# First ConvFFN of a two-layer hybrid block: from an interleaved up and down to an up phase of quarter products and a down phase summed in PSUM

## The chip, the core and the metric

The kernel runs on one core of a Trainium2 chip. The metric is the device time of one execution in microseconds; a time "before" or "after" is the median over several executions. TensorE multiplies matrices, VectorE (DVE) and ScalarE (ACT) work on tiles elementwise, GpSimd (POOL) does some elementwise work and issues some DMAs, and SyncE (SP) issues most DMAs. SBUF is the on-chip memory, PSUM the banks into which TensorE accumulates.

## The reference, cut to what matters

Two layers follow one another; tokens are 256 context tokens and 1024 latent tokens of width 1024. Layer 0 mixes by attention, layer 1 by a state-space model, whose input projection reads all tokens. Behind each mixer stands the same gated ConvFFN:

```python
def conv_ffn(u, w_up, b_up, conv_w, conv_b, w_down, b_down):
    hdn = dwconv_centered(u @ w_up + b_up, conv_w, conv_b)   # 3 taps along the tokens
    val, gate = jnp.split(hdn, 2, axis=-1)                    # D_FF = 2816 each
    return (val * jax.nn.silu(gate)) @ w_down + b_down

def post_norm_layer(h, y_mix, mods, ln_g, ln_b, ffn):
    h = layer_norm(ALPHA * h + mods[2][:, None] * y_mix, ln_g[0], ln_b[0])
    f = conv_ffn(modulate(h, mods[3], mods[4]), *ffn)
    return layer_norm(ALPHA * h + mods[5][:, None] * f, ln_g[1], ln_b[1])   # "LN2" is the outer one
```

Layer 0 needs the ConvFFN for all 1280 tokens, layer 1 for the latents alone. All data are 32-bit floats. Each factor of a product is split into a high part (a copy in TensorE's reduced 32-bit type) and a low part (the rest), and a product is three matmuls: high x high, low x high, high x low.

## The kernel before, in words

The feature dimension of a ConvFFN is cut into 22 blocks of 128 (`NFB`), called feature tiles here, each with a value half and a gate half. The tokens are cut into ten tiles of 128, of which 0 and 1 are context.

**First ConvFFN** (`conv_ffn`). For a feature tile, `up` multiplies the value block and then the gate block of `w_up` with the modulated tokens `uh`, `ul`, in three chunks of 512, 512 and 256 tokens (line 1428, names `wush`, `wusl`). ScalarE copies each chunk from PSUM with the bias. `conv` makes the three taps: one on ScalarE, two on VectorE (L1909 to L1911, tile `cv`). `gated` makes silu on ScalarE and the product on VectorE (L1917), and splits the result into `gh`, `gl`, which stay in SBUF. Between the matmuls of the next tile's `up`, a function `unit` places the down products of the tile before (L1930), twenty of three matmuls, and VectorE adds each result from PSUM into an accumulator `y` in SBUF (L1944). Behind the last tile comes an LN2 stage that is written out by hand: `ffn_out`, `ffn_norm` (L2155 normalizes), the transposes of `emit_u` (L352), and, for each latent tile, the first 512 columns of the SSM's z product (`z_out`, L2186).

**Second ConvFFN** (`lat_up` and `Down`). The latents alone are multiplied in quarters: `w_up`'s block in four quarters (two halves by two halves of the input width), the tokens in four, and seven products in place of eight, from sums `s1` to `s4` of weight quarters and `t1` to `t4` of token quarters (the first three tiles take all eight products, while the sums of the tokens are being made). Each summed quarter needs a high half (`hi`, a ScalarE copy, L1529) and a low half (`lo`, a VectorE subtraction, L1534). The gated tile goes to DRAM (`g1_d`), and `Down` reads it back for groups of four token tiles, whose eight PSUM banks are summed over all 22 feature tiles (L1793).

**Order.** In both parts instructions stand on each engine's queue in the order of the program (`manual_schedule`), and a waiting instruction holds all that stand behind it on its engine. SyncE and GpSimd are such queues too, for the DMAs that they issue. In the background of the first ConvFFN a generator (`gen_ffn0`) places the adaLN products of layer 1 (L266) and then `gen_residual`: GpSimd makes `alpha * h` plus bias terms for ten token tiles (L2035 to L2049), with one tile buffer `t4k`: load from `z_d`, multiply, add, store to `r0_d`. `conv_ffn` takes seven steps of it per block of `up`, two blocks to a feature tile.

**What the change touches.** `up_mul`, `FirstBlock`, `FirstPair`, `lat_up` (lines 1426 to 1742), `Down` (L1744 to L1817), `conv_ffn` and the LN2 stage (L1835 to L2248), the block list and the z blocks of the in-projection (L2531, L2629, L2652), and the call of the second ConvFFN (L2948).

Of the kernel before, what the change touches and what calls it, by code (L numbers as in the profile page):

```python
# [74 lines left out]
def body(nc, tc, a, out):  # L75
# [330 lines left out]
    r0_d = dp.tile([NTOK, D], F32, name="r0d")  # L406
# [1019 lines left out]
    def up_mul(pt, w, uh, ul, k, o, n):  # L1426
        for j, (w_, u_) in enumerate(((w[0], uh), (w[0], ul), (w[1], uh))):
            T.matmul(pt, lhsT=w_[:, k, :], rhs=u_[:, k, o:o + n], start=(k + j == 0), stop=(k == KB - 1 and j == 2))  # L1428

    class FirstBlock:  # L1430

        def __init__(self, pool, l, chunks):
            self.pool, self.src, self.chunks, self.pts = pool, a['ffn_w_up'][l], chunks, []

        def load(self):
            self.raw = self.pool.tile([P, KB, P], F32, name="wuf")
            dma(out=self.raw, in_=self.src.rearrange("(k p) n -> p k n", p=P)[:, :, 0:P])

        def split(self):
            self.hl = [self.pool.tile([P, KB, P], F32R, name="wus" + c) for c in "hl"]  # L1440
            split(*self.hl, self.raw, eng=G)

        def product(self, ci, uh, ul):

            o, n = self.chunks[ci]
            self.pts.append(pp.tile([P, 512], F32, name="mm", bufs=4))
            for k in range(KB):
                up_mul(self.pts[ci][:, :n], self.hl, uh, ul, k, o, n)


    class FirstPair:

        def __init__(self, pool, l, chunks):
            self.pool, self.src, self.chunks, self.pts = pool, a['ffn_w_up'][l].rearrange("(k p) n -> p k n", p=P), chunks, []

        def load(self):
            self.raw = [self.pool.tile([P, KB, P], F32, name="wu" + c) for c in "vg"]
            for i in range(2):
                dma(out=self.raw[i], in_=self.src[:, :, i * DFF:i * DFF + P])

        def split(self):
            self.hl = {}
            for j, nm in enumerate(("a11", "a12")):
                self.hl[nm] = [self.pool.tile([P, 4, P], F32R, name=nm + c) for c in "hl"]
                split(*self.hl[nm], self.raw[0][:, 4 * j:4 * j + 4, :], eng=G)

        def product(self, ci, uh, ul):
# [14 lines left out]
    def lat_up(l, uh, ul, c0, pre, g_d, gq, plain, dpool, ones_ahead):  # L1482
# [20 lines left out]
        raw, A, ops, cv = {0: pre.raw}, {}, {}, {}
        ops[0] = dict(pre.hl)

        def load(n):
            if n < NFB:
                raw[n] = [pre.pool.tile([P, KB, P], F32, name="wu" + c) if n % 2 == 0 else rpool.tile([P, KB, P], F32, name="wu" + c) for c in "vg"]
                for i in range(2):
                    dma(out=raw[n][i], in_=w3[:, :, i * DFF + n * P:i * DFF + (n + 1) * P])  # L1510

        def src(n, nm):
            if nm[0] == 'a':
                return raw[n]['12'.index(nm[1])][:, 4 * '12'.index(nm[2]):4 * '12'.index(nm[2]) + 4, :]
            return A[n, nm]

        def summed(n, nm):

            if n < NFB and n not in plain:
                x, y, f = {'s1': ('a21', 'a22', ALU.add), 's2': ('s1', 'a11', ALU.subtract), 's3': ('a11', 'a21', ALU.subtract), 's4': ('a12', 's2', ALU.subtract)}[nm]  # L1520
                A[n, nm] = rpool.tile([P, 4, P], F32, name="s", bufs=3)
                V.tensor_tensor(out=A[n, nm], in0=src(n, x), in1=src(n, y), op=f)

        def hi(n, nm):
            if n < NFB:
                pool = pre.pool if nm in ('a11', 'a12') else opool
                t = [pool.tile([P, 4, P], F32R, name=('s1' if nm == 'a21' else nm) + c) for c in "hl"]
# [1581 lines left out]
```

## Time and profile before

| | |
|---|---|
| median of 3 executions | 3134.17 us (3133.34 to 3135.21) |
| the profiled execution | 3128.95 us, span 3127.0 us, mean granted TensorE clock 0.979 |
| TensorE busy | 2990.9 us, 96% |
| VectorE busy | 2188.2 us, 70% |
| ScalarE busy | 1276.2 us, 41% |
| GpSimd busy | 686.7 us, 22% |
| first ConvFFN and LN2 stage | first up product at 858, last at 1817, in-projection from 1911 us on |
| second ConvFFN, up phase | 2438 to 2861 us, its feature tiles from 2513 on without a wait of TensorE |

An engine's busy time is a sum over the whole span; what a stage is bound by has to be read from that stage. "Idle before" of a group names the instruction that ended the wait. Matmuls overlap, so a single one's duration (0.39 us for 512 columns) is longer than the pitch at which they follow each other. The granted clock is a share of TensorE's full 2.4 GHz, and its other level is 1.2 GHz.

### The profile page before, as it was taken

To read this page: it belongs to the slowest core of one execution; us is meant where nothing else is said; L and a number is where in the kernel's file an instruction comes from. 1 tells how busy PE (TensorE), PEld (TensorE's weight loads), DVE (VectorE), ACT (ScalarE), POOL (GpSimd) and SP (SyncE) were. 2 spreads that over 40 slices of the span, in tenths; PEclk is the share of its full clock that TensorE was granted. 3 is DMA by queue.
4 is the path that set the end of the run, shared out by engine and by line. 5 is a ranking of instruction groups with operands and counts; after the bars stand their busy time and mean duration, and the time that the engine had idled before them with its cause. 6 is when DMAs were issued, how large, how long until landed. Compare 5 with 4: busy or idle time off the path is not lost.

```text
span 3127.0 us, 39837 instructions
## 1 busy us (share of the span) xinstructions
PE 2990.9 (96%) x15188; PEld 2420.9 (77%) x15188; DVE 2188.2 (70%) x3270; ACT 1276.2 (41%) x2176; POOL 686.7 (22%) x664
## 2 busy tenths in 40 slices
PE   8999999999999999999999969999879999999998
PEld 4776788898888877887788858786648788887786
DVE  2278867887755656565676694966988788886776
ACT  3421257785532222222222345244435555554342
POOL 1046511321100000000442250213654000001412
PEclk9999999999999999999999989999889999999999
DMA  8635569333332222222332233331043222223653
GB/s 277 216 108 162 175 177 210 94 85 110 121 102 81 75 70 79 81 78 64 102 121 81 68 106 96 95 95 43 1 141 101 80 82 81 83 85 120 224 169 108
DMA packets 284883, 347.85 MB, mean 111 GB/s; under 512 B 24135, under 2 KB 207861, under 8 KB 284692
## 3 DMA queue, kind: packets, MB, share of 16 engines
q1 hardware_dynamic: 266820, 289.15, 30.6%
q0 software_dynamic: 11808, 40.94, 3.7%
q10 hardware_dynamic: 6064, 15.21, 1.6%
q8 instruction: 120, 1.97, 0.3%
q14 instruction: 71, 0.58, 0.1%
HBM read 264.74 MB, written 74.20 MB: 108 GB/s over the span
## 4 chain that ended last, share of the span: by engine, by line
PE 75%; DVE 14%; DMA 4%; ACT 3%; issue 2%; POOL 0%; SPq 0%; ACTq 0%; DVEq 0%; POOLq 0%
PE mm L1428 18%; PE mm L1478 12%; PE tr L1930 6%; PE mm L1353 6%; PE mm L2657 4%; PE bg L1930 3%; PE mm L878 3%; PE s L1094 3%; PE mm L1793 3%; PE bg L1152 3%; PE mm L978 2%; PE tr L1793 1%; PE bg L1793 1%; PE bg L266 1%; PE bg L1131 1%
## 5 line engine op out<-in xcount | busy, mean ns | idle before, releaser
L1428 PE MATMUL mm<-uh,wush 128*128 128x512 f32 (+1 forms) x1056 | 378.1, 358 | 0.0
L1428 PE MATMUL mm<-uh,wusl 128*128 128x512 f32 (+1 forms) x1056 | 374.6, 355 | 2.2 <-DVE wusl L90 2.1
L1428 PE MATMUL mm<-ul,wush 128*128 128x512 f32 (+1 forms) x1056 | 375.1, 355 | 0.0
L1889 ACT ACTIVATE hb<-mm,ffc 128x512 f32<-128x512 f32 x132 | 80.9, 614 | 559.3 <-PE mm L1428 559.3
L1944 DVE TENSOR_TENSOR y<-y,tr 128x512 f32<-128x512 f32 x266 | 181.3, 686 | 153.7 <-PE tr L1930 152.9
L1428 PEld LDWEIGHTS mm<-uh,wush 128*128 128x128 f32 x1056 | 199.2, 189 | 57.2 <-issue 23.6
L1428 PEld LDWEIGHTS mm<-ul,wush 128*128 128x128 f32 x1056 | 199.1, 189 | 35.2
L1428 PEld LDWEIGHTS mm<-uh,wusl 128*128 128x128 f32 x1056 | 198.9, 188 | 31.8 <-DVE wusl L90 3.0
L1102 DVE TENSOR_REDUCE mx<-s 128x1 f32<-128x1280 f32 x120 | 150.6, 1272 | 49.8 <-PE s L1094 49.8
L1944 DVE TENSOR_TENSOR y<-y,bg 128x512 f32<-128x512 f32 x134 | 91.8, 685 | 89.8 <-PE bg L1930 89.7
L2028 POOL DMA_DIRECT2D g<-in_ln_g_dram x1 | 0.6, 599 | 623.1 <-DVE y L1944 623.1
L1107 ACT ACTIVATE p<-s,mx 128x1280 f32<-128x1280 f32 x96 | 127.9, 1332 | 19.1 <-DVE r L1112 13.0
L978 PE MATMUL mm<-uh,wsh 128*128 128x512 f32 (+1 forms) x320 | 125.7, 393 | 0.0
L1152 PE MATMUL bg<-vt,wt 128*128 128x128 f32 x960 | 125.5, 278 | 0.0
L372 DVE TENSOR_TENSOR ul<-utmp,uh 128x512 fp32r<-128x512 f32 x76 | 55.1, 747 | 91.2 <-ACT uh L370 91.0
L1152 PEld LDWEIGHTS bg<-vt,wt 128*128 128x128 f32 x960 | 116.6, 193 | 0.7
L978 PE MATMUL mm<-ul,wsh 128*128 128x512 f32 (+1 forms) x320 | 114.5, 358 | 0.0
L978 PE MATMUL mm<-uh,wsl 128*128 128x512 f32 (+1 forms) x320 | 114.4, 357 | 0.0
L1930 PE MATMUL tr<-wdsh,gh 128*128 128x512 f32 x280 | 110.8, 396 | 0.0
L1930 PE MATMUL tr<-wdsl,gh 128*128 128x512 f32 x280 | 109.6, 392 | 1.2 <-DVE wdsl L90 1.2
L1930 PE MATMUL tr<-wdsh,gl 128*128 128x512 f32 x280 | 110.7, 396 | 0.0
L1553 POOL DMA_DIRECT2D g1d<-cvv x22 | 11.8, 537 | 441.8 <-DVE cvv L1552 441.8
(824 smaller groups left out, 8559.2 us busy)
## 6 DMA issues: line engine op xcount, KB each, us to landing
adaw<-in_ada_w_dram SPq DMA_DIRECT2D x40, 1024.0 KB
wdf<-in_ffn_w_down_dram SPq DMA_DIRECT2D x66, 512.0 KB
wuf<-in_ffn_w_up_dram SPq DMA_DIRECT2D x44, 512.0 KB
wuv<-in_ffn_w_up_dram SPq DMA_DIRECT2D x22, 512.0 KB
wug<-in_ffn_w_up_dram SPq DMA_DIRECT2D x22, 512.0 KB
g1d<-cvv POOLq DMA_DIRECT2D x22, 512.0 KB, 2.9
gf<-g1d SPq DMA_DIRECT2D x44, 256.0 KB
wf<-in_attn_w_in_dram SPq DMA_DIRECT2D x18, 512.0 KB
```

The source lines that it names most:

```text
L878: T.matmul(pt[:, :n], lhsT=u_[:, tt, k, :], rhs=w_[:, k, o:o + n], start=(i == 0), stop=(i == 23))
L978: T.matmul(pt.rearrange("p (t n) -> p t n", n=P), lhsT=w_[:, k, :], rhs=u_[:, o // P:(o + n) // P, k, :], start=(k + i == 0), stop=(k == K ...
L1102: V.reduce_max(t.mx[:, i, q:q + 1], t.s[i][:, c0:c0 + nk], axis=X, negate=True)
L1107: S.activation(t.p[i][q], t.s[i][:, c0:c0 + nk], AF.Exp, bias=t.mx[:, i, q:q + 1], accum_out=t.sm[:, i, q:q + 1])
L1152: T.matmul(t.po[:, P:2 * P], lhsT=t.wt[0][:, b, :], rhs=vt[:, b, :], start=(b == 0), stop=(b == NTT - 1))
L1353: T.matmul(pt, lhsT=u_[:, k, :], rhs=w_[k][:, hc], start=(k + i == 0), stop=(k == K - 1 and i == 2))
L1428: T.matmul(pt, lhsT=w_[:, k, :], rhs=u_[:, k, o:o + n], start=(k + j == 0), stop=(k == KB - 1 and j == 2))
L1478: T.matmul(pt, lhsT=w_[:, k, :], rhs=u_[:, k, :], start=start and k + j == 0, stop=stop and k == 3 and j == 2, skip_group_check=True)
L1793: T.matmul(pt, lhsT=g_[:, c], rhs=w_[:, hc], start=start and i == 0, stop=stop and i == 2)
L1930: T.matmul(pt, lhsT=g_[:, c0:c0 + P], rhs=w_[:, hc], start=(start and j == 0), stop=(stop and j == 2))
L1944: V.tensor_tensor(out=yacc[ti][:, hc], in0=yacc[ti][:, hc], in1=pt, op=ALU.add)
L2657: T.matmul(pt[0:M, :n], lhsT=w_[:, k, :], rhs=u_[:, k, o:o + n], start=(k + i == 0), stop=(k == KB - 1 and i == len(pairs) - 1))
```

## The change

The first ConvFFN takes the two-phase form of the second. `lat_up` becomes `ffn_up`, which both call.

- Up: the latents take the seven quarter products (all eight in the first three tiles), and the 256 context tokens are multiplied beside them with the four plain quarters (`ctx`). Weights are loaded by quarters (`up_quarter`). `hi` and `lo` become one function, `parts`, and are called at other places of the tile; the buffers of the operands are a ring of four (`oh`, `ol`).
- The gated tile goes to DRAM (`g0_d`) over GpSimd's queue. The background generator is stepped six times per feature tile from tile 3 on, and what is left of it is run out in the last tile (`for _ in bg: pass`), ahead of the loads for down.
- Down: `Down` takes the token tiles in groups of 4, 3 and 3 (0 to 3, 4 to 6, 7 to 9), each sum over 22 feature tiles staying in PSUM. As a tile is done, its gate and residual are put in (`tile_done`), and LN2 with its transposes is stepped between the matmuls of the next group (`gen_tile`). The first loads of `Down` are followed by one split before up ends, not two; this holds for the second ConvFFN too.
- The first two u blocks of the in-projection, for token tiles 0 to 5, are multiplied at the end of this stage (`early`), and the in-projection makes all six z blocks instead of two.

```diff
-        def hi(n, nm):
+        def parts(n, nm):
             if n < NFB:
...
                 S.activation(t[0], src(n, nm), AF.Copy)
-
-        def lo(n, nm):
-            if n < NFB:
-                t = ops[n][nm]
                 V.tensor_tensor(out=t[1], in0=src(n, nm), in1=fr(t[0]), op=ALU.subtract)
...
+        def ctx(pt, w, j, step=lambda: None):
+
+            if cx:
+                quarter(pt, w, [t[:, 4 * j:4 * j + 4, cx] for t in (uh, ul)], j == 0, j == 1, step)
...
         for n in range(len(plain), NFB):
...
+            silu(n - 1)
+            C = ctx_bank()
+            ctx(C, w['a11'], 0)
+            parts(n, 's3')
+            tick()
             quarter(Wb, w['a12'], U['b21'], True, True)
-            lo(m, 'a11')
+            if m < NFB:
+                parts(m, 'a11')
             gated(n - 1)
...
+            if end:
+                rp.__exit__(None, None, None)
+                if close_raw:
+                    close_raw()
+                if bg:
+                    for _ in bg:
+                        pass
+                down = dpool()
+            load(n + 2, 'a21', 'a22')
+            tick()
+            quarter(Y, w['s4'], U['b22'], False, True)
+            add(0, 1, Y)
+            tap(n, 0)
+            parts(m, 's1')
+            conv(n, 0)
...
     def gen_ffn0():
-        yield
-        yield from gen_ada(1, range(12), "bgb", side_bank, 3, 6, one=True)
+        yield from gen_ada(1, range(12), "bgb", side_bank, 3, 4, one=True)
         yield from gen_residual()
...
+        order = [[0, 1, 2, 3], [4, 5, 6], [7, 8, 9]]
+        dn = Down(0, g0_d, [[(t, gcol(t)) for t in ts] for ts in order], (3, 3, 3), 4)
+        for p in ffn_up(0, uh, ul, NCTX, slice(0, NCTX), pre, g0_d, (0, 1, 2), 0.45, "right", lambda: praw.__exit__(None, None, None),
+                        lambda: dn.start(tc.tile_pool(name="dn0", bufs=1)), gen_ffn0()):
+            p.__exit__(None, None, None)
...
+        def tile_done(t, half, pt):
+            h, hc = hs[t], slice(half * 512, half * 512 + 512)
+            V.tensor_tensor(out=pt, in0=pt, in1=gates[t >= 2][:, hc], op=ALU.mult)
+            V.scalar_tensor_tensor(out=h[:, hc], in0=h[:, hc], scalar=1.0, in1=pt, op0=ALU.mult, op1=ALU.add,
+                                   accum_out=stt[half][:, t:t + 1])
+            if half == 1:
+                work.append(gen_tile(t))
...
+        dn.run(bank, tile_done, step)
+
+        for b in range(2):
+            for ci in range(2):
+                o, n = CH[ci]
+                pt = early[b, o] = pp.tile([P, 512], F32, name="mm", bufs=4)
...
-        blocks = [('u', 0), ('u', 1), ('d', 0), ('x', 6), ('x', 7)] + [('x', i) for i in range(6)] + [('x', 8), ('x', 9), ('z', 4), ('z', 5)]
+        blocks = [('u', 0), ('u', 1), ('d', 0), ('x', 6), ('x', 7)] + [('x', i) for i in range(6)] + [('x', 8), ('x', 9)] + [('z', i) for i in range(6)]
```

The order of instructions on the engines moves at three places that the prediction speaks of. In the rows below a line number is followed by the operation, the tile written, and the tiles read.

**VectorE in a feature tile of the second ConvFFN.** `a11l`, `s1l` and the like are low halves, `s` the sums of weight quarters, `hbv` and `hbg` the value and gate rows to which a product in PSUM is added, `cvv` and `cvg` the convolved rows. Before, from the gate's convolution on:

```order
L1544 SCALAR_TENSOR_TENSOR cvg<-hbg,ffc_101,cvg 128x1024 x2
L1534 TENSOR_TENSOR a11l<-wuv,a11h 128x512
L1552 TENSOR_TENSOR cvv<-cvv,cvg 128x1024
L1522 TENSOR_TENSOR s<-wug 128x512
L1562 TENSOR_TENSOR hbv<-hbv,mm 128x512
L1534 TENSOR_TENSOR a12l<-wuv,a12h 128x512
L1522 TENSOR_TENSOR s<-s,wuv 128x512
L1534 TENSOR_TENSOR s2l<-s,s2h 128x512
L1522 TENSOR_TENSOR s<-wuv,wug 128x512
L1534 TENSOR_TENSOR s1l<-s,s1h 128x512
L1522 TENSOR_TENSOR s<-wuv,s 128x512
L1562 TENSOR_TENSOR hbg<-hbg,mm 128x512
```

After the change, from the same point; `ol` is the ring's low half (the first here is `s3`'s, the third `a22`'s):

```order
L1506 TENSOR_TENSOR ol<-s,oh 128x512
L1506 TENSOR_TENSOR a11l<-ra_23512,a11h 128x512
L1524 TENSOR_TENSOR cvv<-cvv,cvg 128x1024
L1534 TENSOR_TENSOR hbv<-hbv,mm 128x512
L1496 TENSOR_TENSOR s<-ra_23462,ra_23464 128x512
L1506 TENSOR_TENSOR a12l<-ra_23514,a12h 128x512
L1506 TENSOR_TENSOR ol<-ra_23314,oh 128x512
L1496 TENSOR_TENSOR s<-s,ra_23512 128x512
L1534 TENSOR_TENSOR hbv<-hbv,mm 128x512
L1506 TENSOR_TENSOR ol<-s,oh 128x512
L1516 SCALAR_TENSOR_TENSOR cvv<-hbv,ffc_100,cvv 128x1024 x2
L1534 TENSOR_TENSOR hbg<-hbg,mm 128x512
```

The low half of `s3` now stands ahead of the product `cvv`, and the low halves of `a12`, `a22` and the value's convolution stand among the sums in another order.

**ScalarE at the same place.** Before:

```order
L1539 ACTIVATE cvg<-hbg,ffc_101 128x1024
L1559 ACTIVATE hbv<-mm,ffc_101 128x512
L1529 ACTIVATE a11h<-wuv 128x512
L1548 ACTIVATE cvg<-cvg 128x1024
L1529 ACTIVATE a12h<-wuv 128x512
L1559 ACTIVATE hbv<-mm,ffc_101 128x512
L1529 ACTIVATE s2h<-s 128x512
L1559 ACTIVATE hbg<-mm,ffc_101 128x512
L1529 ACTIVATE s1h<-s 128x512
```

After; `oh` behind the silu (`cvg<-cvg`) is the high half of `s3`, whose low half is the first row of VectorE above:

```order
L1531 ACTIVATE hbv<-mm,ffc_100 128x512
L1520 ACTIVATE cvg<-cvg 128x1024
L1505 ACTIVATE oh<-s 128x512
L1505 ACTIVATE a11h<-ra_23512 128x512
L1505 ACTIVATE a12h<-ra_23514 128x512
L1531 ACTIVATE hbg<-mm,ffc_100 128x512
L1531 ACTIVATE hbv<-mm,ffc_100 128x512
L1505 ACTIVATE oh<-ra_23314 128x512
L1511 ACTIVATE cvv<-hbv,ffc_100 128x1024
```

The high halves of `a11` and `a12` stood on either side of the silu, and now a copy for the running tile stands behind the silu, and another behind the tap `cvv<-hbv`.

**GpSimd at the end of the first ConvFFN.** Before, the last residual tiles were followed by loads for the LN2 stage (`r`) and its work on `y`:

```order
L2047 TENSOR_TENSOR t4k<-t4k,rr 128x1024
L2049 DMA r0d<-t4k 128x1024
L2044 DMA t4k<-zd 128x1024
L2046 TENSOR_TENSOR t4k<-t4k,g_13033 128x1024
L2047 TENSOR_TENSOR t4k<-t4k,rr 128x1024
L2049 DMA r0d<-t4k 128x1024
L2096 DMA r<-r0d 128x1024 x2
L2091 TENSOR_SCALAR g_14717<-g_14717 128x1024
L2101 TENSOR_TENSOR y<-y,g_14717 128x1024
```

After, from the gated tile 20 (`g0d<-cvv`) to the gated tile 21; `t4k` is the residual's one buffer, and the two tiles are the context tokens':

```order
L1525 DMA g0d<-cvv 128x1282
L1864 DMA t4k<-in_ln_b_dram 128x1024
L1876 TENSOR_TENSOR rr<-rr,t4k 128x1024
L1880 DMA t4k<-zd 128x1024
L1882 TENSOR_TENSOR t4k<-t4k,g_12165 128x1024
L1883 TENSOR_TENSOR t4k<-t4k,rr 128x1024
L1885 DMA r0d<-t4k 128x1024
L1880 DMA t4k<-zd 128x1024
L1882 TENSOR_TENSOR t4k<-t4k,g_12165 128x1024
L1883 TENSOR_TENSOR t4k<-t4k,rr 128x1024
L1885 DMA r0d<-t4k 128x1024
L1525 DMA g0d<-cvv 128x1282
```

The residual of the two context tiles now stands between the stores of the last two gated tiles. On ScalarE the first split for down (`gh<-gf`, `wdh<-wdf`) stands ahead of the silu of the last tile:

```order
L1531 ACTIVATE hbv<-mm,ffc_99 128x512
L1505 ACTIVATE oh<-ra_12840 128x512
L1511 ACTIVATE cvv<-hbv,ffc_99 128x1282
L1531 ACTIVATE hbg<-mm,ffc_99 128x512
L1531 ACTIVATE hbg<-tr,ffc_99 128x256
L1511 ACTIVATE cvg<-hbg,ffc_99 128x1282
L1784 ACTIVATE gh_13356<-gf 128x512
L1785 ACTIVATE wdh_13354<-wdf 128x1024
L1520 ACTIVATE cvg<-cvg 128x1282
L1784 ACTIVATE gh_13412<-gf 128x512
```

## Rows read from the trace of the kernel before

**Rows 1.** The chain that ended last: shares of the span by engine.

```profile
PE 75%; DVE 14%; DMA 4%; ACT 3%; issue 2%; POOL 0%; SPq 0%; ACTq 0%; DVEq 0%; POOLq 0%
```

**Rows 2.** Stretches: length, busy PE, PEld, DVE, ACT, POOL (instructions); clock, DMA share, GB/s.

```profile
950.00:1765.00 815.00, 811.59 (x4029) 658.37 (x4028) 512.44 (x571) 217.28 (x239) 89.98 (x56) 1.00 0.26 82
1765.00:1820.00 55.00, 46.38 (x216) 38.01 (x215) 45.31 (x54) 15.63 (x20) 29.29 (x15) 0.91 0.24 77
1820.00:1911.00 91.00, 71.71 (x314) 57.19 (x313) 83.55 (x182) 59.07 (x115) 39.03 (x18) 0.89 0.31 107
2500.00:2861.00 361.00, 360.93 (x1570) 294.80 (x1569) 292.00 (x372) 187.80 (x263) 10.11 (x19) 1.00 0.25 82
2861.00:2920.00 59.00, 55.56 (x239) 44.03 (x238) 46.35 (x28) 21.47 (x26) 35.56 (x23) 1.00 0.66 232
```

**Rows 3.** TensorE's waits, 1765 to 1911 us: total, times, longest.

```profile
PE tr L352 <- ACT y L2155: 16.6, 4, 7.5
PE mm L1930 <- ACT gh L1921: 8.6, 1, 8.6
```

**Rows 4.** Timeline, VectorE, one tile: start, us, line, operation; idle before and releaser.

```profile
2642.33 1.23 DVE L1552 TENSOR_TENSOR cvv<-cvv,cvg 128x1024 f32<-128x1024 f32 x1 [0.53 <-ACT cvg L1548]
2643.47 0.69 DVE L1522 TENSOR_TENSOR s<-wug 128x512 f32<-128x512 f32 x1
2644.07 0.68 DVE L1562 TENSOR_TENSOR hbv<-hbv,mm 128x512 f32<-128x512 f32 x1
...
2646.66 0.69 DVE L1534 TENSOR_TENSOR s2l<-s,s2h 128x512 fp32r<-128x512 f32 x1 [0.70 <-ACT s2h L1529]
...
2651.29 0.69 DVE L1562 TENSOR_TENSOR hbv<-hbv,mm 128x512 f32<-128x512 f32 x1 [0.75 <-PE mm L1478]
...
2653.30 2.60 DVE L1544 SCALAR_TENSOR_TENSOR cvv<-hbv,ffc,cvv 128x1024 f32<-128x1024 f32 x2 [0.71 <-ACT cvv L1539]
...
2657.87 2.61 DVE L1544 SCALAR_TENSOR_TENSOR cvg<-hbg,ffc,cvg 128x1024 f32<-128x1024 f32 x2 [0.77 <-ACT cvg L1539]
```

**Rows 5.** The chain in order of time, second ConvFFN: start, us, matmuls.

```profile
2513.27 347.32 PE mm L1478 x1512
```

**Rows 6.** Timeline, TensorE, 256-column matmuls, the first and last of eight.

```profile
1798.73 0.28 PE L1428 MATMUL mm<-ul,wush 128*128 128x256 f32 x1
...
1799.55 0.28 PE L1428 MATMUL mm<-uh,wusl 128*128 128x256 f32 x1
```

**Rows 7.** The chain in order of time, LN2 stage: one z product, one tile's transposes.

```profile
1892.08 5.59 PE bg L2186 x24
1897.67 0.87 PE tr L352 x8
```

**Rows 8.** Timeline, ScalarE, the same tile as rows 4.

```profile
2641.23 1.06 ACT L1548 ACTIVATE cvg<-cvg 128x1024 f32<-128x1024 f32 x1 [1.58 <-DVE cvg L1544]
...
2645.99 0.63 ACT L1529 ACTIVATE s2h<-s 128x512 fp32r<-128x512 f32 x1 [2.30 <-DVE s L1522]
...
2652.02 1.24 ACT L1539 ACTIVATE cvv<-hbv,ffc 128x1024 f32<-128x1024 f32 x1 [0.32 <-DVE hbv L1562]
```

**Rows 9.** Timeline, VectorE, first ConvFFN: the convolution of one gate block.

```profile
1511.15 1.55 DVE L1910 SCALAR_TENSOR_TENSOR cv<-hb,ffc,cv 128x1282 f32<-128x1282 f32 x1 [0.62 <-ACT cv L1909]
1512.74 3.56 DVE L1911 SCALAR_TENSOR_TENSOR cv<-hb,ffc,cv 128x1282 f32<-128x1282 f32 x1
```

**Rows 10.** Timeline, GpSimd: residual chain's first load, first and eighth tile, last store.

```profile
1493.00 0.60 POOL L2028 DMA_DIRECT2D g<-in_ln_g_dram  x1 [623.06 <-DVE y L1944]
...
1518.98 2.43 POOL L2046 TENSOR_TENSOR t4k<-t4k,g 128x1024 f32<-128x1024 f32 x1 [3.17 <-DMA t4k<-zd]
...
1617.43 2.40 POOL L2046 TENSOR_TENSOR t4k<-t4k,g 128x1024 f32<-128x1024 f32 x1 [7.22 <-DMA t4k<-zd]
...
1669.59 0.59 POOL L2049 DMA_DIRECT2D r0d<-t4k  x1 [0.30 <-POOL t4k L2047]
```

**Rows 11.** The chain in order of time, the first matmuls behind the wait for `gh`.

```profile
1811.24 2.93 PE mm L1930 x6
```

More of the change, by code (lines that the diff above doesn't have):

```diff
@@ L1424, in out_proj @@
                     fin()
[L1426 to L1433, printed above, removed]
-        def load(self):
[L1436 to L1448, printed above, removed]
@@ L1451, in body, with up_quarter @@
[L1451 to L1459, printed above, removed]
+    def up_quarter(pool, l, n, nm, bufs=1):
+        i, j = int(nm[1]) - 1, int(nm[2]) - 1
+        t = pool.tile([P, 4, P], F32, name="r" + nm, bufs=bufs)
+        dma(out=t, in_=a['ffn_w_up'][l].rearrange("(k p) n -> p k n", p=P)[:, 4 * j:4 * j + 4, i * DFF + n * P:i * DFF + (n + 1) * P])
+        return t
@@ L1773, in split, with start @@
                 V.tensor_tensor(out=t[1], in0=w, in1=fr(t[0]), op=ALU.subtract)
[L1775 to L1778 removed]
+        def start(self, guard):
+            self.guard = guard
+            self.pool = self.pools[0] = guard.__enter__()
             self.load()
@@ L1784, in start, with ahead @@
             yield
-            self.split()
-            self.load()
-            yield
+        def ahead(self, q):
+            if self.nsplit < q + self.ns:
+                self.split()
+                self.load()
         def mul(self, pt, q, j, half, start, stop):
-            wh, wl, gh, gl = self.sl[q]
+            wh, wl, gh, gl = self.parts[q]
             c, hc = slice(j * P, (j + 1) * P), slice(half * 512, half * 512 + 512)
@@ L1803, in run @@
                         self.mul(pts[i], q, i // 2, i % 2, fb == 0, False)
-                        if i in (0, 4) and self.ns < q + len(self.slots):
-                            self.load()
-                            self.split()
-                        step()
+                        if i in (0, nt):
+                            self.ahead(q)
+                        step(gi)
                     q += 1
@@ L1811, in run @@
                         self.mul(pts[i], q + h, i // 2, i % 2, False, h == hold - 1)
-                        if h == 0 and self.ns < q + len(self.slots):
-                            self.load()
-                            self.split()
-                        step()
-                    tile_done(t0 + i // 2, i % 2, pts[i])
+                        if h == 0:
+                            self.ahead(q)
+                        step(gi)
+                    tile_done(group[i // 2][0], i % 2, pts[i])
                 q += hold
@@ L2016, in body @@
-    phy = ExitStack()
-    yp = phy.enter_context(tc.tile_pool(name="ya0", bufs=1, side="right"))
-    yacc = {tt: yp.tile([P, D], F32, name="y", bufs=NTT) for tt in LN2_ORDER}
     w1 = a['ssm_w_in'][0]
@@ L2021, in body @@
     zs_d = dp.tile([NTOK, AW], F32, name="zsd")
+    g0_d = dp.tile([NFB, P, NTOK + 2], F32, name="g0d")
+    phy = ExitStack()
+    r0_d = dp.tile([NTOK, D], F32, name="r0d")
+    early = {}
     def gen_residual():
```

742 lines of the change are left out of this document (258 added, 484 removed).

## The prediction

> **What bounds the kernel now.** I read the chain of waits first, by engine [rows 1]: TensorE holds 75% of it and VectorE 14%. The reader should take from this that a matmul left out is worth its pitch, except where TensorE already waits. Where it waits is in the table of stretches [rows 2]. In the body of the first ConvFFN (950 to 1765 us) TensorE is busy for 811.6 of 815 us, and VectorE has room: 512 of 815. At the end of that stage and in the LN2 stage (1765 to 1911) TensorE is idle for 8.6 + 19.3 = 27.9 us, and its granted clock is 0.91 and 0.89. The waits of that stretch [rows 3] are 16.6 us before the LN2 transposes and 8.6 us for `gh`. In the second ConvFFN's up phase (2500 to 2861) TensorE is never idle, but VectorE is busy for 292 of 361 us, 81%. The fourth thing to see is how thin the margin of that phase is: VectorE's rows of one tile [rows 4] show that its remaining time is already spent on waits of 0.53, 0.70, 0.75, 0.71 and 0.77 us.
>
> **Prices.** The chain has 1512 matmuls of 512 columns in 347.32 us [rows 5]: 0.2297 us each, 19.3 us for a tile of 84. Seven steps of the 256-column form take 0.82 us [rows 6], 0.117 each. An LN2 z product of 24 matmuls takes 5.59 us and eight transposes 0.87 [rows 7].
>
> **What the change takes away.** Seven of eight products for eight tiles of latents in the first ConvFFN leave 228 matmuls of 512 columns fewer in the program: 228 x 0.2297 = -52.4 us, all on TensorE's path. The z columns move from the LN2 stage (8 x 5.59 = 44.7 us) into the SSM in-projection, so the matmuls stay; the moved blocks bring 32 transposes, +3.5. The early u products (48 x 0.2297 + 48 x 0.117 = 16.6 us) only change places. The old LN2 stage goes with its waits: 27.9 us idle, 3.4 in the body, and about 10 for the slow clock (at a mean of 0.9 a fifth of the time is at 1.2 GHz and loses half; 146 us x 0.1 = 15, of which some fell in idle time): -41. If nothing came back, the time would be 3128.95 - 52.4 + 3.5 - 41 = 3039.
>
> **What it adds: the second ConvFFN.** This is the term that I trust most, and nothing in the change's words names it. `parts` now issues a high half on ScalarE and its low half on VectorE in one place, where the old code issued the high half a step ahead. VectorE does the same work in a tile: fifteen 512-column operations at a pitch of 0.60 (2643.47 to 2644.07), two pairs of convolution steps of 2.60 and one product of 1.14 by its pitch [rows 4], 15.3 us. But its order now puts a dependent low half right behind each ScalarE step. By ScalarE's durations [rows 8] the waits are: silu and the next copy, 1.06 + 0.63 = 1.7; tap and copy, 1.24 + 0.63 = 1.9; a copy right after its sum, 0.7; the second tap, 1.3. That is 5.6 us where there were 3.5. The round is 15.3 + 5.6, with 0.2 to 0.4 of hops, about 21.2 us, against 19.3 on TensorE: VectorE becomes the bound, +1.9 a tile, and 18 to 19 tiles give **+35**. The bounds are 0 (some waits overlap each other) and 19 x 2.6 = 50.
>
> **The first ConvFFN's rounds.** Per tile TensorE needs 84 x 0.2297 + 48 x 0.117 = 24.9 us. VectorE's round is 15 x 0.60 + 4 convolution steps of 1.55 [rows 9] + a product of 1.14 x 1282/1024 + the 5.6 us of waits in the same ratio: 9.0 + 6.2 + 1.4 + 7.0, about 23.5. Without company TensorE stays the bound and this costs nothing; the cover is only 1.4 us.
>
> **The residual.** GpSimd's residual chain starts when the adaLN steps are over. Before, it ran freely, from 1493.00 to 1669.59 [rows 10], 177 us with 14.06 a token tile (1518.98 to 1617.43 for seven), and was over 95 us before the stretch at 1765 began. After, adaLN ends early in tile 16 (of 0 to 21), and six tiles of 24.9 are only 149 us. Two token tiles per feature tile make 2 x 14.06 + 0.6 = 28.7 us on GpSimd, and the store of the gated tile (`g0d`) is queued there behind the residual's waiting instructions; the next `cvv` tap waits for that store. So these six tiles go by GpSimd: 6 x 3.8 = 23, of which I take **20**, since the first starts late. Also, GpSimd's operations and VectorE's two-input operations take turns: a convolution step took 3.56 us beside the residual and 1.55 without [rows 9]. The bounds are 0 (the chain keeps ahead of the ticks) and 50 (below).
>
> **The seam to down.** Both context tiles are flushed at the end, and behind the last-but-one `g0d` GpSimd still has a load of 3.8 (a wait as the 3.17 of [rows 10], and an issue of 0.6), an addition of 2.4 and 2 x 14.06: 34 us, while TensorE has about 20 us of the tile left. The first loads of down reuse the residual's memory and wait for it; ScalarE stands at the first `gh` with the last silu queued behind it, and so the last gated tile. Then a load and a split follow, some 7 us by the 8.6 us that TensorE waited for such a chain in the old kernel [rows 3]. Together 14 + 7 = **+21**; bounds 0 and 42 (177 us of chain less 149 of tiles, and twice the 7).
>
> **The rest.** Loading the first quarters late in the first ConvFFN: +3, a landing as the 3.17 us of [rows 10] (0 to 6). The start of down loads two gates and five residual tiles beside the weights. The nearest stretch is the second ConvFFN's down start, where the same is done at 232 GB/s and TensorE is idle for 3.4 of 59 us [rows 2]: **+4** (0 to 10). LN2 inside down: the transposes of a tile wait for a row of reduction, square root and normalization; the old stage paid 16.6 us in four waits [rows 3]. Now three groups end, the matmuls of the next group and the early u products cover most: **+12** (0 to 50, three times the old). The second ConvFFN's down has one split ahead instead of two: +4, about half the chain of 8.6 (0 to 8.6). The in-projection's 32 new transposes wait for their ScalarE copies: +3, some five of 0.63 [rows 8] (0 to 10). After a long wait TensorE runs slow: behind the 8.6 us of idle [rows 3] the first six matmuls took 2.93 us, 0.49 each [rows 11], about 2 us lost; two such stops: +4.
>
> **Sum.** 3039 + 35 + 20 + 21 + 3 + 4 + 12 + 4 + 3 + 4 = 3145, against the profiled execution's 3128.95. The median of the runs shown, 3134.17, is 5.2 above that execution, so against the median I say **3150**, 0.5% slower. The gain is nearly as large as the losses, so the sign rests on the three terms 35, 20 and 21. About 0.2% (6.3 us) is what a measurement of this kernel can tell from no change.
>
> **The rivals.**
> *The sum holds* (chance 0.45, 3135 to 3170): 0.36 slower, 0.08 same, 0.01 faster.
> *The residual is hidden* (0.15). GpSimd's queue runs ahead of the ticks, since nothing but data holds it. It decides at a chain of 149 us: below that neither the stretch nor the flush exists. For it speaks that the chain spent 3.17 and 7.22 us on waits for loads [rows 10], which other traffic may shorten; against it that one buffer `t4k` makes each load wait for the store before it, and that the ticks now hand out its pieces. Time 3150 - 41 = 3109, faster.
> *VectorE's round in the second ConvFFN stays under 19.3 us* (0.12). That needs 2 of the 5.6 us of waits to sink into each other. The phase had 0.4 us of slack at most, which speaks against it. Time 3150 - 35 = 3115: 0.09 faster, 0.03 same.
> *VectorE and GpSimd block each other and VectorE becomes the bound in the first ConvFFN too* (0.18). In a residual tile four GpSimd operations of 2.4 us lie beside a VectorE round of 23.5; a block of 2.0 each, as in the 3.56 against 1.55 [rows 9], makes 31.5, and the blocked GpSimd operations (up to 3.5 instead of 2.4) bring its chain to about 32 too. Decisive from 1.4 us of blocking in a tile on, the cover named above. Six tiles at 32 to 33.5 instead of 28.2 cost 23 to 32, and the flush a few us: about 3181, slower. The Trainium skill (SBUF — State Buffer, the section on SBUF's two separate sides) says that the port pair which VectorE and GpSimd share is an exclusive lock, held for a whole instruction by whichever came first, while the other blocks fully. By that rule this rival would be the rule in every residual tile, and the sum 3181; the trace agrees as to the blocking, with 3.56 us for 1.55 + 2.0, but had VectorE idle for a third of the time, so how often they meet when it is 90% busy no row shows.
> *Anything else* (0.10): 0.02 faster, 0.04 same, 0.04 slower. That the change leaves the products in place is excluded by the order of instructions.
>
> **The numbers.** The predicted time is the first case's. Its range alone is 3135 to 3170. For 8 in 10 I take in the faster cases from 3100 and the slower one to 3195. Faster 0.01 + 0.15 + 0.09 + 0.02 = 0.27; same 0.15; slower 0.36 + 0.18 + 0.04 = 0.58.
>
> **What would show it.** In the second ConvFFN's up phase TensorE idle by about 2 us a tile, with waits for VectorE's low halves, and a tile period near 21.2 instead of 19.3. In the first ConvFFN a period near 24.9 up to tile 15 and near 28 from tile 16 on, and then one wait of about 20 us before the first matmul of down, with the last residual store right ahead of the first `gf`. TensorE's busy time about 50 us less. I am wrong if the second ConvFFN keeps 19.3 us a tile, if down starts without a wait of over 10 us, or if the LN2 transposes wait for more than 30 us in total.

## The result and the profile after

The changed kernel takes 3177.1 us (median of 4 executions, 3174.4 to 3179.7), the kernel before 3131.0 beside it: a ratio of 1.0145, 95% interval 1.0128 to 1.0162. An earlier measurement gave 1.0148 (1.0124 to 1.0172), 3179.56 against 3133.76. So it is slower by 46 us, where 16 were forecast. One execution, the one first profiled, took 7409 us with 512-column matmuls 0.62 us apart in place of 0.23, so all rows below are from another profiled execution of the same kernel, 3179.67 us long, to be held against the 3128.95 of before.

Page of the changed kernel: busy time by engine, and the chain by engine.

```profile
PE 2956.9 (93%) x14992; PEld 2391.5 (75%) x14992; DVE 2131.7 (67%) x3251; ACT 1383.4 (44%) x2422; POOL 644.7 (20%) x667
...
PE 58%; DVE 15%; issue 12%; DMA 6%; ACT 6%; POOL 2%; SPq 1%; ACTq 0%; DVEq 0%; POOLq 0%
```

TensorE does 34 us less work than before, but its share of the chain fell from 75% [rows 1] to 58%: it now waits for others. The stretches show where. First the kernel before (first ConvFFN's body, its end with the LN2 stage, in-projection to the output projection, second ConvFFN's up):

```profile
857.00:1765.00 908.00, 904.59 (x4512) 734.70 (x4511) 560.86 (x631) 255.91 (x292) 90.73 (x65) 1.00 0.26 84
1765.00:1911.00 146.00, 118.09 (x528) 95.19 (x528) 128.86 (x235) 74.70 (x135) 68.32 (x33) 0.89 0.29 96
1911.00:2425.50 514.50, 469.58 (x2325) 366.74 (x2324) 384.54 (x678) 214.01 (x413) 195.34 (x182) 0.94 0.28 81
2425.50:2866.00 440.50, 436.77 (x1921) 356.69 (x1920) 354.79 (x467) 232.68 (x336) 11.27 (x21) 1.00 0.26 81
```

and the changed kernel (first ConvFFN's up, seam, down, early u products, in-projection to output projection, second ConvFFN's up):

```profile
855.00:1488.00 633.00, 610.51 (x3221) 498.38 (x3219) 446.83 (x514) 268.34 (x396) 85.72 (x76) 0.99 0.37 121
1488.00:1518.00 30.00, 0.77 (x1) 0.29 (x1) 9.59 (x6) 4.01 (x4) 12.18 (x7) 0.52 0.36 128
1518.00:1856.00 338.00, 318.42 (x1391) 260.47 (x1392) 174.37 (x297) 151.36 (x236) 17.26 (x17) 0.96 0.55 174
1856.00:1886.00 30.00, 21.39 (x110) 17.60 (x109) 9.80 (x32) 15.89 (x31) 0.00 (x0) 0.89 0.12 39
1886.00:2439.00 553.00, 500.54 (x2449) 389.63 (x2447) 385.02 (x678) 219.81 (x420) 193.82 (x182) 0.95 0.28 81
2439.00:2919.00 480.00, 445.05 (x1919) 357.05 (x1917) 355.36 (x470) 225.79 (x336) 11.28 (x21) 0.99 0.25 79
```

The first ConvFFN with LN2, up to the in-projection's first own matmul, went from 1053 us to 1030. That is a gain of 24 us, where the prediction's steps for this part sum to a gain of 57. The next stretch is longer by 39 us (35 forecast), the second ConvFFN's up by 39.5 (35 and 4 forecast). TensorE's waits from the seam to the end of LN2 (total, times, longest), which answer to [rows 3]:

```profile
PE tr L1809 <- ACT wdh L1785: 30.2, 1, 30.2
PE tr L351 <- ACT z L1959: 25.4, 6, 8.7
```

Two causes hold most of it: one wait of 30.2 us in the seam between up and down, and six waits before LN2's transposes.

### The profile page after: what moved, and what is told of

The parts are those of the page before. It is cut to its first block, busy times and chain, and to the rows that moved or that the text cites. A ratio compares the mean times of both kernels' runs of the same rounds, so it can differ in the third digit from the quotient of the medians.

```text
span 7407.4 us, 40544 instructions
## 1 busy us (share of the span) xinstructions
PE 7370.7 (100%) x14992; PEld 4727.4 (64%) x14992; DVE 2053.5 (28%) x3251; ACT 1423.1 (19%) x2422; POOL 596.7 (8%) x667
## 4 chain that ended last, share of the span: by engine, by line
PE 99%; DVE 0%; DMA 0%; ACT 0%; issue 0%; POOL 0%; SPq 0%; DVEq 0%; ACTq 0%
PE mm L1456 30%; PE mm L1809 11%; PE mm L2418 8%; PE mm L1351 7%; PE mm L976 7%; PE bg L1809 5%; PE tr L1456 4%; PE s L1092 4%; PE bg L1150 4%; PE tr L1809 3%; PE mm L876 3%; PE bg L1129 2%; PE bg L265 2%; PE tr L351 1%; PE tr L2492 1%; PE mm L2549 1%
## 5 line engine op out<-in xcount | busy, mean ns | idle before, releaser
L1809 PE MATMUL mm<-wdh,gh 128*128 128x512 f32 x440 | 367.5, 835 | 0.0
L1809 PE MATMUL mm<-wdl,gh 128*128 128x512 f32 x440 | 364.6, 829 | 0.0
L1809 PE MATMUL mm<-wdh,gl 128*128 128x512 f32 x440 | 362.6, 824 | 0.0
L1456 PE MATMUL mm<-uh,oh 128*128 128x512 f32 x400 | 331.7, 829 | 0.0
L1456 PE MATMUL mm<-ul,oh 128*128 128x512 f32 x400 | 331.5, 829 | 0.0
L1456 PE MATMUL mm<-uh,ol 128*128 128x512 f32 x400 | 329.7, 824 | 0.0
L1150 PE MATMUL bg<-vt,wt 128*128 128x128 f32 x960 | 309.2, 537 | 0.0
L2418 PE MATMUL mm<-uh,wxh 128*128 128x512 f32 (+1 forms) x320 | 256.8, 803 | 0.0
L2418 PE MATMUL mm<-ul,wxh 128*128 128x512 f32 (+1 forms) x320 | 247.2, 772 | 0.0
L2418 PE MATMUL mm<-uh,wxl 128*128 128x512 f32 (+1 forms) x320 | 246.1, 769 | 0.0
```

The lines of the kernel that those rows point to most:

```text
L1150: T.matmul(t.po[:, P:2 * P], lhsT=t.wt[0][:, b, :], rhs=vt[:, b, :], start=(b == 0), stop=(b == NTT - 1))
L1456: T.matmul(pt, lhsT=w_[:, k, :], rhs=u_[:, k, :], start=start and k + j == 0, stop=stop and k == 3 and j == 2, skip_group_check=True)
L1809: T.matmul(pt, lhsT=g_[:, c], rhs=w_[:, hc], start=start and i == 0, stop=stop and i == 2)
L2418: T.matmul(pt[0:M, :n], lhsT=w_[:, k, :], rhs=u_[:, k, o:o + n], start=(k + i == 0), stop=(k == KB - 1 and i == len(pairs) - 1))
```

## Experiments

Theory A is the prediction's main case. Theory B is its rival in which VectorE and GpSimd block each other. Theory C puts the loss into down. The first run was the changed kernel again:

> The changed kernel itself once more, for a trace that shows its stages at the time of its median. Theory A (the three terms of the prediction: VectorE's round in the second ConvFFN +35, GpSimd's residual chain +20, the seam to down +21): 3165 to 3190 us, feature tiles of the second ConvFFN at 21.2 us, of the first at 24.9 up to tile 15 and 28 behind it, one wait of some 20 us before down. Theory B (VectorE and GpSimd block each other): tiles 16 to 21 of the first ConvFFN at 32 us or more, with waits for VectorE. Theory C (the time was lost inside down, to LN2 and loads): waits of TensorE of over 40 us in the groups of down.

Measured: 3177.1 us. VectorE's timeline of one feature tile of the second ConvFFN, which answers to [rows 4] (start, duration, line, operation; idle before):

```profile
2641.13 0.69 DVE L1506 TENSOR_TENSOR ol<-s,oh 128x512 fp32r<-128x512 f32 x1 [0.76 <-ACT oh L1505]
...
2644.34 2.60 DVE L1516 SCALAR_TENSOR_TENSOR cvg<-hbg,ffc,cvg 128x1024 f32<-128x1024 f32 x2 [1.31 <-ACT cvg L1511]
2648.59 0.69 DVE L1506 TENSOR_TENSOR ol<-s,oh 128x512 fp32r<-128x512 f32 x1 [1.65 <-ACT oh L1505]
...
2656.46 0.69 DVE L1506 TENSOR_TENSOR ol<-s,oh 128x512 fp32r<-128x512 f32 x1 [1.83 <-ACT oh L1505]
...
2662.35 0.69 DVE L1506 TENSOR_TENSOR ol<-s,oh 128x512 fp32r<-128x512 f32 x1 [0.76 <-ACT oh L1505]
```

The period is 2662.35 - 2641.13 = 21.2 us, and the waits are 0.76 + 1.31 + 1.65 + 1.83 = 5.55: the 5.6 and 21.2 of the prediction. TensorE's waits in that up phase, 17 of 1.65 us in the mean, where 1.9 a tile were forecast:

```profile
PE mm L1456 <- ACT hbg L1531: 28.0, 17, 2.2
```

In a residual tile of the first ConvFFN VectorE's timeline shows the same operations at 0.64 us each (the row with two) and at 2.3 to 3.3:

```profile
1379.07 3.30 DVE L1496 TENSOR_TENSOR s<-ra,ra 128x512 f32<-128x512 f32 x1
1382.29 2.87 DVE L1506 TENSOR_TENSOR a12l<-ra,a12h 128x512 fp32r<-128x512 f32 x1
1385.08 1.28 DVE L1506 TENSOR_TENSOR ol<-ra,oh 128x512 fp32r<-128x512 f32 x2
...
1393.32 0.68 DVE L1534 TENSOR_TENSOR hbg<-hbg,mm 128x512 f32<-128x512 f32 x1
1393.92 2.29 DVE L1506 TENSOR_TENSOR ol<-s,oh 128x512 fp32r<-128x512 f32 x1
1396.24 2.77 DVE L1496 TENSOR_TENSOR s<-ra,s 128x512 f32<-128x512 f32 x1
```

Beside it GpSimd's timeline:

```profile
1378.85 0.53 POOL L1525 DMA_DIRECT2D g0d<-cvv  x1 [8.74 <-DVE cvv L1524]
1379.40 2.41 POOL L1882 TENSOR_TENSOR t4k<-t4k,g 128x1024 f32<-128x1024 f32 x1
1381.89 2.72 POOL L1883 TENSOR_TENSOR t4k<-t4k,rr 128x1024 f32<-128x1024 f32 x1
...
1392.55 3.11 POOL L1882 TENSOR_TENSOR t4k<-t4k,g 128x1024 f32<-128x1024 f32 x1 [3.38 <-DMA t4k<-zd]
1395.74 2.73 POOL L1883 TENSOR_TENSOR t4k<-t4k,rr 128x1024 f32<-128x1024 f32 x1
...
1411.27 0.53 POOL L1525 DMA_DIRECT2D g0d<-cvv  x1 [8.73 <-DVE cvv L1524]
```

Each of four VectorE operations is stretched where a residual operation runs, by 2.6, 2.2, 1.7 and 2.1 us over its pitch of 0.60, some 8.6 in all, and each ends 0.54 to 0.56 us behind the GpSimd operation beside it. The period is 32.4 us (1378.85 to 1411.27): VectorE is busy for 26.0 us of it, blocks included, and waits 6.3 us for ScalarE. GpSimd waits 8.7 us for the gated product in each of these tiles. So GpSimd's queue is not the bound here, as theory A had it; VectorE is, lengthened by blocks, as theory B had it.

**The second ConvFFN alone** (e1). `parts` is split into `hi` and `lo` again. The copies for `a11`, `s1` and `s3` are issued ahead of silu and the taps, and a tap or a sum stands between the high and the low half of `s1`, `s4` and `s3`. The lines below are the branch taken in the second ConvFFN; the conditions are cut:

```diff
...
+                hi(m, 'a11')
+                lo(m, 'a11')
             silu(n - 1)
...
-            tap(n, 0)
-            parts(m, 's1')
+                hi(m, 's1')
+                tap(n, 0)
+                lo(m, 's1')
...
-            parts(m, 's4')
-            summed(m, 's3')
+                hi(m, 's4')
+                summed(m, 's3')
+                lo(m, 's4')
...
-            tap(n, 1)
+                hi(m, 's3')
+                tap(n, 1)
+                lo(m, 's3')
```

> In the second ConvFFN alone the high halves are issued ahead of silu and taps again, with the low halves filling the waits. Theory A: about 35 us less than the changed kernel, near 3145, feature tiles of the second ConvFFN back at 19.3 to 19.6 us. If VectorE's round is not the bound there: no change, 3180.

Measured: 3140.4 us, ratio 1.0034 (1.0021 to 1.0047): 37 us less than the changed kernel, and the second ConvFFN's up phase alone is 36 us shorter (475.5 to 439.3). GpSimd's timeline has the stores of two gated tiles, 19.32 us apart:

```profile
2632.88 0.53 POOL L1534 DMA_DIRECT2D g1d<-cvv  x1 [18.79 <-DVE cvv L1533]
2652.20 0.53 POOL L1534 DMA_DIRECT2D g1d<-cvv  x1 [18.79 <-DVE cvv L1533]
```

So the order in which the two halves of an operand are issued cost 37 us: this is shown.

**The residual first** (e3):

```diff
-        yield from gen_ada(1, range(12), "bgb", side_bank, 3, 4, one=True)
         yield from gen_residual()
+        yield from gen_ada(1, range(12), "bgb", side_bank, 3, 4, one=True)
```

> The background runs the residual first and the adaLN products behind it, so that down starts behind no residual. Theory A: the seam's 21 us go, and the stretched tiles move to the front but stay: near 3158. Theory B: six tiles at 32 us now at the front (tiles 3 to 8), time 3155 to 3165. Theory C: no change, 3180.

Measured: 3165.6 us, ratio 1.0105 (1.0088 to 1.0123). TensorE's timeline, last matmul of up and first of down:

```profile
1494.63 0.28 PE L1456 MATMUL tr<-uh,ol 128*128 128x256 f32 x1
1498.47 0.76 PE L1809 MATMUL tr<-wdh,gh 128*128 128x512 f32 x1 [3.57 <-issue]
```

The seam is 3.6 us long in place of 30.2, so the residual made 26.6 of it. The up phase grew by 9 us (640.5 from 631.4). All ten token tiles of the residual now lie in it, and behind them TensorE waits as long as the whole growth for adaLN's first weights:

```profile
PE bg L265 <- DMA adaw<-in_ada_w_dram: 9.1, 1, 9.1
```

SyncE held that load for 8.4 us, until the residual's last store was done. The sum, 17, lies between the 12 of the medians and the 24 of the two profiled executions. The residual's feature tiles still take 30.8 us at the front, where theory A had 28: that speaks for B.

**No residual** (e4): `gen_residual` is not called, and LN2 loads `z_d` in place of `r0_d`.

> The residual's GpSimd work is left out: LN2 adds the attention output's tile as it was stored in place of alpha * h plus bias, so the output differs. Theory A: 41 us less, near 3138. Theory B: 60 to 70 us less, near 3115, since the blocks go as well. Theory C: no change, 3180.

Measured: 3116.2 us, ratio 0.9955 (0.994 to 0.997): 61 us less than the changed kernel, where A had 41 and B 60 to 70. The stretch of one feature tile without residual and adaLN:

```profile
1366.90:1391.98 25.08, 25.08 (x133) 21.49 (x132) 17.70 (x22) 11.83 (x18) 0.54 (x2) 1.00 0.22 69
```

25.08 us with TensorE busy throughout: the 24.9 of the prediction. Against this 32.4 us is 7.3 more in each of the residual's tiles; the up phase is 31.5 us shorter than the changed kernel's (599.9 from 631.4) and the seam 26.6.

**The first ConvFFN too** (e2), with e1's edit in both; only in the first the copy of `a11` stays behind silu.

> As e1, but the high halves are issued ahead in the first ConvFFN too. VectorE's round there should fall by about 4.5 us of waits (silu 1.3, copy 0.6, tap 0.6 twice, s4 0.7 and so on). If VectorE, lengthened by blocks, is the bound of tiles 16 to 20 (theory B), these go from 32.4 to about 28 and the time is 18 to 24 us below e1, near 3118. If GpSimd's queue is the bound of these tiles (theory A's mechanism), they stay at 32.4 and the time is e1's, 3140. Tiles without residual: no change under either.

Measured: 3131.6 us, ratio 0.9995 (0.9985 to 1.0004): 9 us below e1 by the medians and 12 by the ratios, about half of what was expected. GpSimd's timeline, stores of two gated tiles:

```profile
1372.80 0.53 POOL L1534 DMA_DIRECT2D g0d<-cvv  x1 [6.06 <-DVE cvv L1533]
...
1403.05 0.53 POOL L1534 DMA_DIRECT2D g0d<-cvv  x1 [6.98 <-DVE cvv L1533]
```

The period is 30.25 us, not 28 and not 32.4. The round became shorter by 2.2 us only: VectorE's waits for ScalarE fell from 6.3 to 4.0, and the one for `a11`'s high half, which the edit leaves behind silu here, stayed (1.86 us). That the period moved at all speaks against GpSimd's queue as the bound; its wait for the gated product is still 6 to 7 us.

**e2 with the residual first** (e5).

> e2 with the residual first. The seam's 30 us of TensorE idle shrink to under 5, as they did when the residual ran first: 15 to 25 us below e2, near 3098, and below the kernel before by about 1%. If the time of the seam only moves (to a wait for adaLN's end): no change against e2.

Measured: 3124.4 us, ratio 0.9971 (0.9959 to 0.9984): 7 us below e2. The seam fell from 33.6 to 3.6 us and the up phase grew by 18. Most of that growth is again TensorE's wait for adaLN's first weights:

```profile
PE bg L265 <- DMA adaw<-in_ada_w_dram: 13.7, 1, 13.7
```

So the second branch of the expectation, that the time moves to adaLN, held for about half of the seam.

**LN2 later** (e6), with two more steps ahead of the square root, five more ahead of the transposes, and a step per unit from the second group on:

```diff
-            yield
-            yield
+            for _ in range(4):
+                yield
...
                 dma(out=z2_d[t * P:(t + 1) * P, :], in_=h)
-            yield
-            yield
-            yield
+            for _ in range(8):
+                yield
...
-            if gi == 2 or units[0] % 2 == 0:
+            if gi >= 1 or units[0] % 2 == 0:
                 forth(work)
```

> The changed kernel with LN2 stepped once per unit from the second group on and five more steps between normalization and transposes. Theory C: most of the 25 us that transposes wait for the normalized tile go, and with them some slow clock: 15 to 25 us less than the changed kernel, near 3157. If the wait is ordered by VectorE's queue of weight splits whatever the steps: less than 8 us, near 3172.

Measured: 3163.4 us, ratio 1.0092 (1.0073 to 1.0111): 14 us less than the changed kernel. TensorE's waits, seam to in-projection:

```profile
PE tr L351 <- ACT z L1959: 11.0, 5, 4.4
PE mm L2417 <- ACT cx L2327: 7.5, 1, 7.5
```

The waits for the normalized tile fell from 25.4 to 11.0 us and down from 338 to 323; 5.9 came back as a longer wait of the in-projection (7.5, from 1.6). So the loss in down was LN2 in part: theory C holds for a share of about 15 us of the 46.

**The residual on VectorE** (e7), with the three operations that prepare its row `rr` (cut below):

```diff
...
-                    G.tensor_tensor(out=zt, in0=zt, in1=g1, op=ALU.mult)
-                    G.tensor_tensor(out=zt, in0=zt, in1=t, op=ALU.add)
+                    V.tensor_tensor(out=zt, in0=zt, in1=g1, op=ALU.mult)
+                    V.tensor_tensor(out=zt, in0=zt, in1=t, op=ALU.add)
```

> The residual's multiplications and additions are on VectorE in place of GpSimd, the DMAs stay. Theory B: in a residual tile the blocks (8.5 us) go and four operations of about 1.2 come, so 32.4 becomes about 28.6, five tiles give 19 us, and the chain at the seam is shorter by 5 to 10: near 3150. Without any blocking the work alone would make VectorE's round 4.8 us longer: 3177 or more.

Measured: 3160.8 us, ratio 1.0091 (1.0076 to 1.0106): 16 us less. Stores of two gated tiles on GpSimd's timeline:

```profile
1411.89 0.53 POOL L1525 DMA_DIRECT2D g0d<-cvv  x1 [10.19 <-DVE cvv L1524]
...
1440.62 0.53 POOL L1525 DMA_DIRECT2D g0d<-cvv  x1 [10.17 <-DVE cvv L1524]
```

28.73 us, as expected. VectorE is faster with four operations more in its tile than with the same four on GpSimd beside it. This tells the block from mere lateness: the work did not shrink, it moved to the busier engine. The time stayed 11 us above the 3150 expected. The seam became 10 us shorter (20.1), but the up phase only 3.9: ahead of the residual's tiles VectorE now stands for 7.7 us before the preparation of `rr`, and that feature tile takes 35.0 us instead of 28.1.

```profile
1330.36 1.22 DVE L1871 TENSOR_TENSOR rr<-rr,t4k 128x1024 f32<-128x1024 f32 x1 [7.71 <-issue]
```

**All four edits** (e8), and the same with the residual left on GpSimd (e9).

> High halves ahead in both ConvFFNs, residual first and on VectorE, LN2 later. By the terms measured one by one: second ConvFFN -37, seam -26, LN2 -14, residual tiles from 32.4 to about 26 (six, -38), minus what overlaps: 3080 to 3100 us, 1.0 to 1.6% below the kernel before. If the gains exclude each other (each only uncovers the next): no better than e5, 3124.

> The same with the residual left on GpSimd: it differs from e8 by the blocks alone. Theory B: tiles with residual at about 29 to 30 us in place of 26, so 15 to 25 us above e8, 3105 to 3112. If the blocks hide behind the shorter round: the same as e8.

Measured: e8 3104.7 us, ratio 0.9908 (0.9893 to 0.9923); e9 3114.6, ratio 0.9939 (0.9926 to 0.9951). Both beat the kernel before, and e8 misses the 3080 to 3100 expected. The 10 us between them are not the price of the blocks, though e9 was to show it. Stores of two gated tiles on GpSimd's timeline, e8 first, then e9:

```profile
1009.98 0.53 POOL L1534 DMA_DIRECT2D g0d<-cvv  x1 [8.76 <-DVE cvv L1533]
...
1040.87 0.53 POOL L1534 DMA_DIRECT2D g0d<-cvv  x1 [8.76 <-DVE cvv L1533]
```

```profile
1042.17 0.54 POOL L1534 DMA_DIRECT2D g0d<-cvv  x1 [0.77 <-DVE cvv L1533]
...
1071.01 0.54 POOL L1534 DMA_DIRECT2D g0d<-cvv  x1 [0.77 <-DVE cvv L1533]
```

A residual tile takes 30.9 us with the work on VectorE (e8) and 28.8 with it on GpSimd (e9). In e9 GpSimd's wait for the gated product is down to 0.77 us: with the high halves ahead and the residual first, its own chain nearly sets the period, at the 28.7 us that theory A had counted for it. What e9 loses comes behind these tiles, where TensorE waits for adaLN's first weights, 13.6 us against 3.6 in e8:

```profile
PE bg L265 <- DMA adaw<-in_ada_w_dram: 13.6, 1, 13.6
```

And of the 12 us between the two profiled executions 4.7 lie before the first ConvFFN, where their code is the same. That e8's tiles are not at 26 us is due to a wait of VectorE, here in four of them:

```profile
DVE t4k L1917 <- DMA t4k<-zd: 17.1, 4, 4.6
```

On VectorE's queue the residual waits for its load, 17.1 us in four times, which GpSimd's queue had borne.

**e8 with the loads ahead** (e10): a tile's load is issued behind the store before it.

> e8 with each residual tile's load issued right behind the store before it, three steps ahead of its use in place of one. In e8 VectorE waits 4.4 us per feature tile for that load, and its residual tiles take 30.8 us. If that wait is what kept them above 26, they fall to 26 to 27 and the time to 3078 to 3090. If VectorE's round with the added work is what bounds them: no change, 3105.

Measured: 3093.5 us, ratio 0.9878 (0.9861 to 0.9894), 11 us below e8 and 1.2% below the kernel before: the fastest run here, though above the 3078 to 3090 expected. The residual's tiles came to 26 to 30 us, and the same wait is still there, shorter:

```profile
DVE t4k L1918 <- DMA t4k<-zd: 12.8, 4, 3.9
```

With one buffer a tile's load can start only behind the store before it; a second buffer was not tried.

## Why the prediction was wrong in size

The forecast was a loss of 16 us and the loss was 46. Three terms of the sum were too small: the residual's tiles (20, measured 31.5), the seam (21, measured 30.2), and the start of down with LN2 and the slow clock (4 + 12 + 4, measured 39). In the first the mechanism was wrong too.

- **Second ConvFFN, +35: right.** Period 21.2 us and waits of 5.55 as worked out; e1 gives 37 back. The rival in which the round stays under 19.3 fell.
- **Residual's tiles, +20: wrong in mechanism and size.** The step that failed is "these six tiles go by GpSimd". GpSimd waits 8.7 us in each. The blocks do it: 32.4 us a tile, within the 32 to 33.5 that the blocking rival gave, and 31.5 us in all by e4. The rule of the Trainium skill (SBUF — State Buffer, the section on SBUF's two separate sides) that one of the two engines waits for the other's whole instruction agrees with these rows: 3.30 us for an operation of 0.68 beside one of 2.41. Which of the two came first does not come out of that row: by the record that VectorE operation began 0.33 us ahead of GpSimd's and was held even so. I gave that rival 0.18 because the old trace, with VectorE idle for a third of the time, did not show how often the two would meet; with VectorE busy for 26.0 of 32.4 us, blocks included, all four residual operations of the tile met one of its own.
- **Seam, +21: right in mechanism, short by 9.** GpSimd's last residual store, ScalarE's first split and TensorE's first matmul of down:

```profile
1508.36 0.59 POOL L1885 DMA_DIRECT2D r0d<-t4k  x1 [0.30 <-POOL t4k L1883]
```

```profile
1514.11 0.63 ACT L1784 ACTIVATE gh<-gf 128x512 fp32r<-128x512 f32 x1 [23.45 <-DMA gf<-g0d]
1516.08 1.06 ACT L1785 ACTIVATE wdh<-wdf 128x1024 fp32r<-128x1024 f32 x1 [1.33 <-DMA wdf<-in_ffn_w_down_dram]
```

```profile
1517.23 0.77 PE L1809 MATMUL tr<-wdh,gh 128*128 128x512 f32 x1 [30.16 <-ACT wdh L1785]
```

  The order is as forecast. GpSimd's chain was even shorter than the 34 us forecast: 31.8, from the end of the store of gated tile 20 (1477.20) to the end of the last residual store's issue (1508.95). What failed is "TensorE has about 20 us of the tile left": it had 9.9, since its last matmul of up ended at 1487.07. The load and the split behind the chain took 8.3, not 7. 31.8 - 9.9 + 8.3 = 30.2. With the residual out of the way 3.6 us remain.
- **Down start 4, LN2 12, slow clock 4: right in kind, half the size.** Down and the early products take 338 + 30 us; their matmuls and transposes by the prices of the prediction are 1320 x 0.2297 + 16.6 + 8.7 = 328.5, so 39 are lost, not 20. Waits before LN2's transposes are 25.4 of it, in six stops with the longest 8.7. I had taken the 16.6 of the old stage as mostly covered; but the normalization's small VectorE steps stand behind the weight splits of the next group, as VectorE's timeline shows ahead of the longest stop:

```profile
1756.79 1.23 DVE L1787 TENSOR_TENSOR wdl<-wdf,wdh 128x1024 fp32r<-128x1024 f32 x1 [2.07 <-ACT wdh L1785]
1757.94 0.15 DVE L129 TENSOR_SCALAR rsxb<-st 128x1 f32<-128x1 f32 x1
```

  `rsxb`, the first step of the square root, comes behind a split that waited for ScalarE, which waited for the weights (1.57 us). The granted clock of 0.96 over 338 us makes up to 13 of the rest, as 338 x 0.04.
- **First quarters, +3: small, as forecast.** e4's up phase of 599.9 us is 2 us above its matmuls at the prediction's prices (598 with adaLN).
- **What leaves: right, by the program.** TensorE's busy time is 34 us less instead of about 50, probably since matmuls at the slow clock count longer; that was not tested. The in-projection's stretch grew by 39, not 35; the runs above, with the same code there, take 546 to 554 us, a spread that stays unexplained.
- **Tile period before the residual: 28.3, not 24.9.** I had forgotten the adaLN products in these tiles. They are in the kernel before as well, so the sum did not move.

Sum of the misses: 11.5 in the residual's tiles, 9 in the seam, 19 in down, 4 in the in-projection, 43.5 together. Against them stand 5 that the old stage had lost beyond the 41 counted: its 1053 us less its matmuls at the same prices (485 + 124 up, 303 down, 45 z, 9 transposes, and 41 for adaLN, 13 tiles by 28.3 - 25.1) leave 46. That is 38.5, against 35 (50.9 by the spans, 16 forecast).

That the blocking rival's 3181 us is near the measured time is partly chance: its mechanism accounts for some 11 us over the main case, and the seam and LN2 for the rest.

## What to carry to other kernels

When two phases are merged into shared code, count the slower engine's round anew, operation by operation, with each wait for the engine that feeds it: the high and low half of an operand issued in one place instead of two cost 37 us here, against the 52 that the left-out products saved. A VectorE that was idle for a third of the time absorbed GpSimd's work beside it; beside a VectorE that bounds the tile, 11 us of the same work cost 7.3 us a tile. A background chain that must end before a seam has to be started so early that its own time fits, and put on a queue where its waits hold nothing that is due. What it then holds up in its turn counts as well: adaLN's weights, held for the residual's last store, cost 3.6 to 13.7 us.

## What the runs showed of the hardware

Two things were new to me. A VectorE operation on two SBUF inputs that began beside a GpSimd one was held to its end (3.30 and 2.87 us beside operations of 2.41 and 2.72), in all four meetings of the tile; one with an input in PSUM beside the same work kept its 0.68 (`hbg` at 1393.32, in the rows of run again). And moving GpSimd's four operations onto the bounding VectorE made the tile shorter, 28.7 us against 32.4; but with the high halves ahead and the residual first it made the tile longer, 30.9 against 28.8, since VectorE then waited for the loads.
